# Decay matrices with dt in the exponent, made two heads ahead, in a state-space layer on one Trainium2 core

## The chip, the cores and the metric

One core of one Trainium2 chip runs the program. The time is the device time of one execution in microseconds (us). A run of a kernel is many executions; the table below has the median of three runs. The rows further down come from one execution that the hardware profiler recorded. Engines are named as in the profile: PE (matrix products), PEld (its weight loads), DVE (VectorE), ACT (ScalarE), POOL (GpSimd) and SP (SyncE, which issues the DMAs). Each engine works through its own list of instructions in order.

## What is computed

One layer of a diffusion backbone: 512 tokens with 1024 channels and 256 context tokens. An input projection feeds a convolution module and a bidirectional state-space mixer (SSD); both branches are projected, gated and added, and a squared-ReLU MLP follows. The part that the change touches is, for each direction and each of 32 heads, over chunks of 128 tokens:

```python
cum = jnp.cumsum(dts * a.astype(F32).reshape(g, r), axis=2)
xdt = x5 * dts[..., None]
seg = cum_t[..., :, None] - cum_t[..., None, :]
decay = jnp.exp(jnp.where(lower, seg, -jnp.inf))
cb = jnp.einsum('bcqgn,bckgn->bcgqk', cs_, bs)
y_diag = jnp.einsum('bcgrqk,bckgrp->bcqgrp', cb[:, :, :, None] * decay, xdt)
...
y_off = jnp.einsum('bcqgn,bcgrpn,bcqgr->bcqgrp', cs_, h_in, jnp.exp(cum))
```

`y_diag` needs one 128x128 decay matrix for each head, direction and chunk; `y_off` needs C scaled by exp(cum). In the convolution module the gate is `glu[..., :CONV_DIM] * sigmoid(glu[..., CONV_DIM:])`.

## The kernel before

Channels lie on the partitions, tokens along the rows. Every dense product runs as three passes over high and low parts (`gemm`, lines L114, L115 and L116 of the profile): a weight tile `raw` is loaded by SP, ACT casts it to `whi` (L105), DVE subtracts to get `wlo` (L106), and PE does 24 products of 128x512 for each tile of 128 output channels (128x256 for the context).

Eight groups of four heads follow each other. `proj(g)` makes B, C, x and Z of a group (short convolution on DVE, L374). `ssd(g)` makes B^T C of the four chunks in PSUM (`cps`, L442), two masked copies `cbm` (DVE, L446), B and x by token (L454, L465, L470), the states `sps` on PE (L485) and the scan over chunks `hst` on DVE (L497, L498). Then, for each pair of heads (j) and each head of it (r) and direction (d):

- SP loads `cfb`, two rows of 512 numbers (cum and exp(cum)) spread over all partitions, 512 KB.
- ACT does four Relu (L510) and one Exp (L512) into `e`, DVE multiplies by `cbm` (L513).
- Direction 0: ACT multiplies by dt chunk by chunk (L517). Direction 1: DVE multiplies by dt and adds both directions, four instructions of 128x128 (L520).
- `Cd` = C times exp(cum): on POOL for six of eight in a group, on DVE for direction 0, second head (L523).

PE then does 32 narrow products into `yps` (16 from `Cd` and `hst`, L536, 16 from `e`, L532), DVE finishes `yt` (L540, L541). Products of the next group's projection and of the convolution module stand between these on PE; the convolution's taps run on DVE (L575).

The order in each engine's list is made at build time from a running number in which `later(n)` moves what it holds. Tiles come from pools whose tags have a fixed number of buffers: a tile that takes over a buffer waits for the last reader of the tile that had it. `Cd` of direction 0 has three buffers in the pool `tp`, `Cd` of direction 1 has four in `spool`.

Of the kernel before, what the change touches and what calls it, by code (L numbers as in the profile page):

```python
# [14 lines left out]
P = 128  # L15
# [11 lines left out]
# columns of the packed per-channel vectors  # L27
# [8 lines left out]
# order of the input projection's 128-column tiles  # L36
# [6 lines left out]
# the groups beside which the first tiles of the convolution module run  # L43
GLU_AT = (0, 1, 2, 3, 4)
# [12 lines left out]
def build(tc, xT, ctxT, cond, crow, wada1, wada2, vecs, hv, cst, w_in, w_co, w_so, w_o, w_1, w_2, outT):  # L57
    nc = tc.nc
    with ExitStack() as es:
# [70 lines left out]
        def rsqrt_mean(ps, n, cnt, r=None):  # L130
            """1/sqrt(sum/cnt + EPS) of a sum broadcast over the partitions"""
# [18 lines left out]
        def rsqrt_rows(parts, n, cnt, pool, out=None):  # L150
            """the same of the sum of several tiles, found token by token and then spread over the partitions"""
# [40 lines left out]
        with tc.tile_pool(name="st", bufs=1) as st:  # L192
# [31 lines left out]
            # products of nothing: the tensor engine's clock halves when it idles  # L224
# [52 lines left out]
        nc.sync.dma_start(C[:, 2:], cst[:, 2:])  # L277
# [16 lines left out]
        def dt_part(ps, pc):  # L294
            conv = bigt("conv")
            # rows: heads forward, the same again, heads backward, the same again; the first of each hold
            # chunks 0 to 2, the second chunk 3 and the context
# [40 lines left out]
            nc.vector.tensor_tensor(wg, wg, dt_, ALU.mult)  # L338
            nc.scalar.activation(ecf, cf, AF.Exp)
# [5 lines left out]
            # step s: chunk s forward, chunk 3 - s backward  # L345
# [4 lines left out]
            for src, dst in ((wg, wgT), (cf, cfT), (dt_, dtT)):  # L350
# [36 lines left out]
        def xbc_first():  # L387
            """the first group's, all of x's part before ctx's"""
# [25 lines left out]

        def proj(g):
# [20 lines left out]

        def ssd(g, Bt, Ct, X, Z):
            ch = lambda t, c: t[:, c * P:(c + 1) * P]
            # B^T C of every chunk, for both directions
# [59 lines left out]
            # outputs of the heads, two to a PSUM tile  # L499
            for j in range(2):  # L500
                yps = py.tile([P, T], F32, name="yps", tag="py")
                Ms, Cs = [], ([], [])
                for r in range(2):
                    for d in range(2):
                        hd = d * HEADS + 4 * g + 2 * j + r
                        cb_ = spool.tile([P, 2, T], F32, name="cfb", tag="cfb", bufs=3)
                        nc.sync.dma_start(cb_, s_cf[hd].unsqueeze(0).broadcast_to([P, 2, T]))
                        e = (spool if d else tp).tile([P, T], F32, name="e", tag="e" if d else "M", bufs=2 if d else 3)
                        for c in range(NCH):
                            nc.scalar.activation(  # L510
                                ch(e, c), cb_[:, 0, c * P:(c + 1) * P], AF.Relu, bias=cfT[:, c, hd:hd + 1], scale=-1.0)
                        nc.scalar.activation(e, e, AF.Exp, scale=-1.0)  # L512
                        nc.vector.tensor_tensor(e, e, cbm[d].rearrange("p c q -> p (c q)"), ALU.mult)  # L513
                        if d == 0:
                            M = e
                            for c in range(NCH):
                                nc.scalar.activation(ch(M, c), ch(M, c), AF.Copy, scale=dtT[:, c, hd:hd + 1])  # L517
                        else:
                            for c in range(NCH):
                                nc.vector.scalar_tensor_tensor(  # L520
                                    ch(M, c), ch(e, c), dtT[:, c, hd:hd + 1], ch(M, c), ALU.mult, ALU.add)
# [355 lines left out]
```

## Time and profile before

| | |
|---|---|
| median of 3 runs | 1266.08 us (1263.03 to 1270.63) |
| span of the profiled execution (the page lists no other time of it) | 1264.2 us |
| PE busy | 1220.7 us, 97% of the span |
| DVE busy | 953.7 us, 75% |
| ACT busy | 667.4 us, 53% |
| POOL busy | 108.9 us, 9% |
| stretch of the eight groups | about 97 to 600 us |

Read it so: PE is busy nearly all the time, so its idle time by stretch and what ended it is what a change on other engines can alter. Shares of the whole span hide that DVE's work is not spread evenly over the stages.

### The profile page before, as it was taken

Reading aid. Unit: us, or ns where it says so; the run is one execution under the profiler, and the core shown is the slowest. Engines: PE = TensorE matmul, PEld = TensorE weight load, DVE = VectorE, ACT = ScalarE, POOL = GpSimd, SP = SyncE. Lnnn points to the kernel's source line nnn. Section 1 sums busy time; section 2 is a strip of 40 time slices with the busy share of each in tenths; the row PEclk is TensorE's granted clock in tenths of the full one; section 3 lists DMA queues with packets and bytes.
Section 4 is the critical chain, followed back from the end, with each engine's and each line's share of the span. In section 5 each row is a group of like instructions: output and inputs, shape, how many; then the busy total and the mean of one; then the engine's idle time right before and its main releaser. Section 6 shows DMA issues by size and latency. Waiting matters only on the chain.

```text
span 1264.2 us, 17493 instructions
## 1 busy us (share of the span) xinstructions
PE 1220.7 (97%) x6665; PEld 995.6 (79%) x6665; DVE 953.7 (75%) x1567; ACT 667.4 (53%) x1124; POOL 108.9 (9%) x74
## 2 busy tenths in 40 slices
PE   6998999999999899999999999999999999999997
PEld 3786778777787778787888877778998888888886
DVE  6797689999999999998999798885843343443444
ACT  4557888686776748868453452134431331331442
POOL 0001222121020302124000000000000000000000
PEclk8999999999999999999999999999999999999999
DMA  9424363343342424333363357964222333233332
GB/s 363 142 67 133 137 198 128 120 146 106 121 159 93 158 83 147 112 134 117 109 193 126 119 188 258 305 196 153 62 65 86 100 100 92 92 100 101 96 104 67
DMA packets 56260, 169.96 MB, mean 134 GB/s; under 512 B 6640, under 2 KB 9584, under 8 KB 56048
## 3 DMA queue, kind: packets, MB, share of 16 engines
q1 hardware_dynamic: 56176, 168.85, 41.0%
q8 instruction: 52, 0.85, 0.3%
q14 instruction: 32, 0.26, 0.1%
HBM read 162.27 MB, written 6.55 MB: 134 GB/s over the span
## 4 chain that ended last, share of the span: by engine, by line
PE 65%; DVE 20%; DMA 8%; issue 3%; ACT 3%; SPq 0%; POOL 0%; DVEq 0%; ACTq 0%; POOLq 0%
PE ps L114 20%; PE ps L115 19%; PE ps L116 19%; DVE conv L575 5%; DVE wlo L106 3%; DVE Xt L374 3%; DMA aw<-in_wada_dram 2%; DMA cfb<-s_cf 2%; PE yps L536 2%; PE yps L532 2%; PE sps L485 1%; DMA yr<-s_y 1%; DVE aw L675 1%; DMA raw<-in_w_dram 1%; ACT whi L105 1%
## 5 line engine op out<-in xcount | busy, mean ns | idle before, releaser
L105 ACT CAST whi<-raw 128x1024 fp32r<-128x1024 f32 x163 | 170.9, 1049 | 320.6 <-PE ps L115 291.5
L106 DVE TENSOR_TENSOR wlo<-raw,whi 128x1024 fp32r<-128x1024 f32 x163 | 203.8, 1251 | 84.3 <-ACT whi L105 76.1
L114 PE MATMUL ps<-hh,whi 128*128 128x512 f32 x632 | 258.0, 408 | 2.3 <-DVE Xt L374 2.1
L116 PE MATMUL ps<-hh,wlo 128*128 128x512 f32 x632 | 255.4, 404 | 2.3 <-DVE wlo L106 2.2
L115 PE MATMUL ps<-hl,whi 128*128 128x512 f32 x632 | 256.7, 406 | 0.0
L575 DVE SCALAR_TENSOR_TENSOR conv<-sg,V,conv 128x480 f32<-128x480 f32 (+14 forms) x240 | 173.3, 740 | 2.6 <-ACT conv L569 1.1
L114 PEld LDWEIGHTS ps<-hh,whi 128*128 128x128 f32 x632 | 119.4, 189 | 30.8 <-issue 7.2
L116 PEld LDWEIGHTS ps<-hh,wlo 128*128 128x128 f32 x632 | 119.4, 189 | 30.7 <-DVE wlo L106 4.7
L115 PEld LDWEIGHTS ps<-hl,whi 128*128 128x128 f32 x632 | 119.6, 189 | 26.5 <-issue 3.7
L711 DVE SCALAR_TENSOR_TENSOR x<-ps,mod,x 128x512 f32<-128x512 f32 (+1 forms) x48 | 31.7, 660 | 100.1 <-PE ps L116 100.1
L510 ACT ACTIVATE e<-cfb,cfT 128x128 f32<-128x128 f32 x256 | 83.9, 391 | 36.8 <-PE yps L532 17.5
L523 POOL TENSOR_TENSOR Cd<-Ct,cfb 128x512 f32<-128x512 f32 x48 | 72.6, 1518 | 313.0 <-DMA cfb<-s_cf 250.3
L116 PE MATMUL ps<-h2h,wlo 128*128 128x512 f32 (+1 forms) x240 | 89.8, 375 | 0.0
L115 PE MATMUL ps<-h2l,whi 128*128 128x512 f32 (+1 forms) x240 | 89.8, 375 | 0.0
L114 PE MATMUL ps<-h2h,whi 128*128 128x512 f32 (+1 forms) x240 | 89.4, 375 | 0.0
L115 PE MATMUL ps<-gl,whi 128*128 128x512 f32 x224 | 88.4, 395 | 0.0
L114 PE MATMUL ps<-gh,whi 128*128 128x512 f32 x224 | 88.2, 394 | 0.0
L116 PE MATMUL ps<-gh,wlo 128*128 128x512 f32 x224 | 87.9, 392 | 0.0
L374 DVE SCALAR_TENSOR_TENSOR Xt<-ps,V,Xt 128x255 f32<-128x255 f32 (+3 forms) x128 | 74.2, 605 | 3.9 <-ACT Xt L370 3.6
L114 PE MATMUL ps<-hc,whi 128*128 128x256 f32 x184 | 52.5, 285 | 3.1 <-DVE Xt L374 3.1
L115 PE MATMUL ps<-hc,whi 128*128 128x256 f32 x184 | 52.4, 285 | 0.0
L116 PE MATMUL ps<-hc,wlo 128*128 128x256 f32 x184 | 52.1, 283 | 0.0
(259 smaller groups left out, 2417.5 us busy)
## 6 DMA issues: line engine op xcount, KB each, us to landing
raw<-in_w_in_dram SPq DMA_DIRECT2D x81, 512.0 KB, 3.6
cfb<-s_cf SPq DMA_DIRECT2D x64, 512.0 KB, 4.4
raw<-in_w_dram SPq DMA_DIRECT2D x64, 512.0 KB, 3.5
aw<-in_wada_dram SPq DMA_DIRECT2D x64, 256.0 KB, 4.3
ablk<-in_wada_dram SPq DMA_DIRECT2D x16, 512.0 KB, 8.6
raw<-in_w_so_dram SPq DMA_DIRECT2D x16, 512.0 KB, 3.7
s_y<-yt SPq DMA_DIRECT2D x16, 256.0 KB, 2.2
yr<-s_y SPq DMA_DIRECT2D x16, 256.0 KB, 3.6
```

Of the source, the lines that this page charges most:

```text
L105: nc.scalar.copy(hi, raw)
L106: nc.vector.tensor_tensor(lo, raw, hi, ALU.subtract)
L114: nc.tensor.matmul(ps, lhsT=whi[:, k, :], rhs=rhi[:, k, t0:t1], start=start and k == 0, stop=False)
L115: nc.tensor.matmul(ps, lhsT=whi[:, k, :], rhs=rlo[:, k, t0:t1], start=False, stop=False)
L116: nc.tensor.matmul(ps, lhsT=wlo[:, k, :], rhs=rhi[:, k, t0:t1], start=False, stop=stop and k == KT - 1)
L374: nc.vector.scalar_tensor_tensor(o[:, lo:hi], ps[:, lo + d:hi + d], vcol(V_SCW + 5 * ch + j), o[:, lo:hi], ALU.mult, ALU.add)
L510: nc.scalar.activation(ch(e, c), cb_[:, 0, c * P:(c + 1) * P], AF.Relu, bias=cfT[:, c, hd:hd + 1], scale=-1.0)
L523: (nc.vector if (d, r) in DECAYS_V else nc.gpsimd).tensor_tensor(Cd, Ct, cb_[:, 1, :], ALU.mult)
L532: nc.tensor.matmul(o, lhsT=xt[:, c, hr, :], rhs=ch(Ms[r], c), start=False, stop=True, skip_group_check=True)
L536: nc.tensor.matmul(o, lhsT=hst[:, s, k, hr * 64:hr * 64 + 64], rhs=ch(Cs[k][r], c), start=k == 0 and c == 0, stop=False, skip_group_check= ...
L575: nc.vector.scalar_tensor_tensor(o[:, :, lo:hi], u[:, :, lo + d:hi + d], wv(j), o[:, :, lo:hi], ALU.mult, ALU.add)
L711: nc.vector.scalar_tensor_tensor(x1[:, j, a:b], ps[:, a:b], mod[:, gcol + j, 0:1], x1[:, j, a:b], ALU.mult, ALU.add)
```

## The change

- `expo` makes the decay matrices by itself, two heads ahead of use (`LEAD = 2`). For each head and direction it loads only the cum row (`E`, 256 KB, L459 of the changed kernel). POOL's `affine_select` writes -1e30 outside the triangle (L463), ACT does four Exp with the bias `bT` = ln(dt) - cum (no Relu, no multiplication by dt), DVE adds the two directions (L468) and, at use, multiplies by `cb`, an unmasked copy of B^T C that ACT makes (L541, L478).
- `Cd` has a DMA of its own for the exp(cum) row, which lands in the `Cd` tile (L537) and is multiplied in place (L538), by POOL or DVE as before. Direction 1 has seven buffers, direction 0 still three.
- `cbm` and the masks are gone, and one of three transposed dt tables; DVE and ACT do a max, a Ln and a subtraction in its place.
- The gate of the convolution is tanh: ACT does Tanh(0.5 x), DVE (tanh + 1) times a, and 0.5 goes into the tap weights once.

```diff
+CDB, EB, LEAD, ADDV, E_LATER, E_LATER0 = 7, 7, 2, 1, 0, 0
...
+            nc.vector.tensor_scalar(dt_, dt_, DT_MIN, None, ALU.max)
+            nc.scalar.activation(dt_, dt_, AF.Ln)
+            nc.vector.tensor_tensor(dt_, dt_, cf, ALU.subtract)
...
-            for src, dst in ((wg, wgT), (cf, cfT), (dt_, dtT)):
+            for src, dst in ((wg, wgT), (dt_, bT)):
...
+        def expo(upto):
...
+                for d in range(2):
+                    hd = d * HEADS + h
+                    e = (tp if d else spool).tile([P, T], F32, name="E", tag="M" if d else "E", bufs=3 if d else EB)
+                    nc.sync.dma_start(e, s_cf[hd, 0].unsqueeze(0).broadcast_to([P, T]))
...
+                    x3 = e.rearrange("p (c q) -> p c q", q=P)
+                    sign = -1 if d else 1
+                    nc.gpsimd.affine_select(x3, x3, pattern=[[0, NCH], [sign, P]], compare_op=ALU.is_ge,
+                                            fill=never, base=0, channel_multiplier=-sign)
+                    for c in range(NCH):
+                        nc.scalar.activation(x3[:, c], x3[:, c], AF.Exp, bias=bT[:, c, hd:hd + 1])
+                    es_.append(e)
+                (nc.vector if ADDV else nc.gpsimd).tensor_tensor(es_[0], es_[0], es_[1], ALU.add)
+                ahead.append(es_[0])
...
-            cbm = []
-            for m in (mask_f, mask_b):
...
+            cb = spool.tile([P, T], F32, name="cb", tag="cb", bufs=1)
+            nc.scalar.copy(cb, cps)
...
-                        cb_ = spool.tile([P, 2, T], F32, name="cfb", tag="cfb", bufs=3)
-                        nc.sync.dma_start(cb_, s_cf[hd].unsqueeze(0).broadcast_to([P, 2, T]))
...
-                        Cd = (spool if d else tp).tile([P, T], F32, name="Cd", tag="Cd", bufs=4 if d else 3)
-                        (nc.vector if (d, r) in DECAYS_V else nc.gpsimd).tensor_tensor(Cd, Ct, cb_[:, 1, :], ALU.mult)
+                        Cd = (spool if d else tp).tile([P, T], F32, name="Cd", tag="Cd", bufs=CDB if d else 3)
+                        nc.sync.dma_start(Cd, s_cf[hd, 1].unsqueeze(0).broadcast_to([P, T]))
+                        (nc.vector if (d, r) in DECAYS_V else nc.gpsimd).tensor_tensor(Cd, Ct, Cd, ALU.mult)
                         Cs[d].append(Cd)
+                    M = ahead.pop(0)
+                    nc.vector.tensor_tensor(M, M, cb, ALU.mult)
                     Ms.append(M)
+                with later(E_LATER):
+                    expo(4 * g + 2 * j + 2 + LEAD)
...
-                nc.scalar.activation(sg, pb, AF.Sigmoid)
+                nc.scalar.activation(sg, pb, AF.Tanh, scale=0.5)
...
-                nc.vector.tensor_tensor(sg, sg, pa, ALU.mult)
+                nc.vector.scalar_tensor_tensor(sg, sg, 1.0, pa, ALU.add, ALU.mult)
```

The order moves at three places that matter below. First, POOL's list at its start, group 0. Before, its first instructions are the `Cd` of the first heads:

```order
L523 TENSOR_TENSOR Cd_1024<-Ct_586,cfb_1011 128x512 [waits DMAHW0_49]
L523 TENSOR_TENSOR Cd_1054<-Ct_586,cfb_1041 128x512 [waits DMAHW2_49]
L523 TENSOR_TENSOR Cd_1099<-Ct_586,cfb_1086 128x512 [waits DMAHW4_49,PE_49]
L523 TENSOR_TENSOR Cd_1114<-Ct_586,cfb_1101 128x512 [waits DMAHW5_49]
L523 TENSOR_TENSOR Cd_1144<-Ct_586,cfb_1131 128x512 [waits DMAHW7_49]
L523 TENSOR_TENSOR Cd_1664<-Ct_1251,cfb_1651 128x512 [waits DMAHW0_49,PE_49,Activation_49]
L523 TENSOR_TENSOR Cd_1679<-Ct_1251,cfb_1666 128x512 [waits DMAHW3_49,PE_49,Pool_49]
```

In the changed kernel seven `affine_select` stand ahead of six `Cd` (the last three of the seven are shown), and two more behind them:

```order
L463 AFFINE_SELECT E_955<-E_955 128x512 [waits DMAHW1_49]
L463 AFFINE_SELECT E_962<-E_962 128x512 [waits DMAHW2_49,DVE_49]
L463 AFFINE_SELECT E_970<-E_970 128x512 [waits DMAHW3_49]
L538 TENSOR_TENSOR Cd_1052<-Ct_587,Cd_1052 128x512 [waits DMAHW3_49,Activation_49]
L538 TENSOR_TENSOR Cd_1055<-Ct_587,Cd_1055 128x512 [waits DMAHW4_49]
L538 TENSOR_TENSOR Cd_1062<-Ct_587,Cd_1062 128x512 [waits DMAHW7_49]
L538 TENSOR_TENSOR Cd_1096<-Ct_587,Cd_1096 128x512 [waits DMAHW1_49,PE_49]
L538 TENSOR_TENSOR Cd_1099<-Ct_587,Cd_1099 128x512 [waits DMAHW2_49]
L538 TENSOR_TENSOR Cd_1106<-Ct_587,Cd_1106 128x512 [waits DMAHW3_49]
L463 AFFINE_SELECT E_1110<-E_1110 128x512 [waits DMAHW4_49]
L463 AFFINE_SELECT E_977<-E_977 128x512 [waits DMAHW5_49,DVE_49]
```

So the first heads' `Cd`, and the last `E` of the first group, come behind more work on POOL.

Second, DVE's list at the first chunk scan of group 0 (`hst`), before:

```order
L470 TENSOR_TENSOR xw1_949<-xps_957,wgT_575 128x256
L470 TENSOR_TENSOR xw0_948<-xps_965,wgT_575 128x256 [waits PE_49]
L470 TENSOR_TENSOR xw1_949<-xps_965,wgT_575 128x512
L497 TENSOR_TENSOR hst_973<-hst_973,decb_576 128x512 [waits DMAHW5_49,Activation_49]
L498 TENSOR_TENSOR hst_973<-hst_973,sps_980 128x512 [waits DVE_49,PE_49]
L497 TENSOR_TENSOR hst_973<-hst_973,decb_576 128x512 [waits DVE_49]
L498 TENSOR_TENSOR hst_973<-hst_973,sps_985 128x512 [waits DVE_49,PE_49]
```

and in the changed kernel:

```order
L541 TENSOR_TENSOR E_940<-E_940,cb_990 128x512
L381 SCALAR_TENSOR_TENSOR Xt_1283<-ps_1314,V_72,Xt_1283 128x254 [waits DVE_49]
L468 TENSOR_TENSOR E_970<-E_970,E_977 128x512 [waits DMAHW3_49,DMAHW5_49,Activation_49,Pool_49]
L541 TENSOR_TENSOR E_955<-E_955,cb_990 128x512
L541 TENSOR_TENSOR E_970<-E_970,cb_990 128x512 [waits DVE_49]
L527 TENSOR_TENSOR hst_1029<-hst_1029,decb_574 128x512 [waits DMAHW6_49,Activation_49]
L111 TENSOR_TENSOR wlo_1416<-raw_1413,whi_1415 128x1024 [waits DMAHW0_49,PE_49,Activation_49]
L528 TENSOR_TENSOR hst_1029<-hst_1029,sps_1036 128x512 [waits DVE_49,PE_49]
```

The scan's first step now stands behind the sum of a head's two directions (which waits for POOL and ACT) and two products with `cb`.

Third, PE's list at the second pair of heads of group 2, where `Cd` of direction 0, second head, takes over the buffer of the first pair's first `Cd` (three buffers, four tiles in a group; names end in the tile's number). Before, the last product that reads the old tile, `Cd_2321`, is the fifth of these rows:

```order
L536 MATMUL yps_2307<-Cd_2321,hst_2285 64x128 [waits DVE_49]
L536 MATMUL yps_2307<-Cd_2351,hst_2285 64x128
L536 MATMUL yps_2307<-Cd_2321,hst_2285 64x128 [waits DVE_49]
L536 MATMUL yps_2307<-Cd_2351,hst_2285 64x128
L536 MATMUL yps_2307<-Cd_2321,hst_2285 64x128 [waits DVE_49]
L536 MATMUL yps_2307<-Cd_2351,hst_2285 64x128
```

and the first that reads the new tile, `Cd_2443`, comes 97 instructions after it, here last but one:

```order
L114 MATMUL ps_2604<-hh_76,whi_2599 128x512
L115 MATMUL ps_2604<-hl_77,whi_2599 128x512
L116 MATMUL ps_2604<-hh_76,wlo_2600 128x512
L114 MATMUL ps_2604<-hh_76,whi_2599 128x512
L536 MATMUL yps_2399<-Cd_2443,hst_2285 64x128 [waits DVE_49]
L536 MATMUL yps_2399<-Cd_2413,hst_2285 64x128
```

In the changed kernel the old tile is `Cd_2266`, read last in the third of these rows:

```order
L555 MATMUL yps_2265<-Cd_2266,hst_2243 64x128 [waits DVE_49]
L555 MATMUL yps_2265<-Cd_2273,hst_2243 64x128
L555 MATMUL yps_2265<-Cd_2266,hst_2243 64x128 [waits DVE_49]
L555 MATMUL yps_2265<-Cd_2273,hst_2243 64x128
L555 MATMUL yps_2265<-Cd_2269,hst_2243 64x128 [waits Pool_49]
L555 MATMUL yps_2265<-Cd_2276,hst_2243 64x128 [waits Pool_49]
```

and the new one, `Cd_2349`, is read first in the last of these:

```order
L555 MATMUL yps_2341<-Cd_2342,hst_2243 64x128 [waits Pool_49]
L119 MATMUL ps_2424<-hh_76,whi_2419 128x512
L120 MATMUL ps_2424<-hl_77,whi_2419 128x512
L121 MATMUL ps_2424<-hh_76,wlo_2420 128x512
L119 MATMUL ps_2424<-hh_76,whi_2419 128x512
L120 MATMUL ps_2424<-hl_77,whi_2419 128x512
L121 MATMUL ps_2424<-hh_76,wlo_2420 128x512
L119 MATMUL ps_2424<-hh_76,whi_2419 128x512
L555 MATMUL yps_2341<-Cd_2349,hst_2243 64x128 [waits DVE_49]
```

So 25 instructions lie between, 18 narrow ones into `yps` and seven products, where there were 97. SP's list at the new tile's load:

```order
L101 DMA raw_2485<-in_w_in_dram 128x1024 [waits DMAHW4_49,DVE_49]
L101 DMA raw_2523<-in_w_in_dram 128x1024 [waits DMAHW5_49,DVE_49]
L537 DMA Cd_2349<-s_cf_575 128x512 [waits PE_49,Pool_49]
L537 DMA Cd_2889<-s_cf_575 128x512 [waits PE_49]
L101 DMA raw_2591<-in_w_in_dram 128x1024 [waits DMAHW1_49,DVE_49]
```

and DVE's at its product:

```order
L594 SCALAR_TENSOR_TENSOR conv_717<-sg_2133,V_72,conv_717 128x8x49 [waits Activation_49]
L594 SCALAR_TENSOR_TENSOR conv_717<-sg_2133,V_72,conv_717 128x8x50 [waits DVE_49]
L559 SCALAR_TENSOR_TENSOR yt_2334<-Xt_1906,V_72,yps_2265 128x512 [waits PE_49]
L538 TENSOR_TENSOR Cd_2349<-Ct_1868,Cd_2349 128x512 [waits DMAHW3_49,Pool_49]
L560 TENSOR_TENSOR yt_2334<-yt_2334,Z_2067 128x512 [waits DVE_49]
L594 SCALAR_TENSOR_TENSOR conv_717<-sg_2133,V_72,conv_717 128x8x51
```

The load itself now waits for PE's last use of the old tile. Before, the numbers came in `cfb`, which has buffers of its own, and only the product waited for the old tile.

## Rows read from the trace of the kernel before

**Rows 1.** The page: span, and busy time of each engine.

```profile
span 1264.2 us, 17493 instructions
PE 1220.7 (97%) x6665; PEld 995.6 (79%) x6665; DVE 953.7 (75%) x1567; ACT 667.4 (53%) x1124; POOL 108.9 (9%) x74
```

**Rows 2.** Windows: stretch and length, busy of PE, PEld, DVE, ACT, POOL; clock; DMA.

```profile
97.00:200.00 103.00, 94.83 (x582) 73.82 (x581) 77.47 (x135) 85.41 (x182) 18.90 (x14) 0.98 0.49 154
200.00:600.00 400.00, 389.74 (x2309) 315.26 (x2309) 383.35 (x618) 292.24 (x542) 81.68 (x52) 1.00 0.38 126
114.00:120.00 6.00, 6.00 (x29) 4.00 (x27) 3.69 (x6) 4.74 (x9) 2.59 (x2) 0.72 0.29 99
129.00:136.00 7.00, 6.18 (x45) 5.05 (x46) 5.53 (x13) 5.76 (x12) 2.07 (x2) 1.00 0.09 37
```

**Rows 3.** What PE waited for, 97 to 200 us: total, times, longest.

```profile
PE yps L536 <- POOL Cd L523: 6.2, 3, 3.1
PE dtp L353 <- DVE conv L338: 1.6, 1, 1.6
```

**Rows 4.** Timeline of PE and POOL in group 0.

```profile
113.69 0.43 PE L536 MATMUL yps<-Cd,hst 128*64 128x128 f32 x2 [3.15 <-POOL Cd L523]
129.82 0.43 PE L536 MATMUL yps<-Cd,hst 128*64 128x128 f32 x2 [1.65 <-POOL Cd L523]
112.37 2.96 POOL L523 TENSOR_TENSOR Cd<-Ct,cfb 128x512 f32<-128x512 f32 x2 [111.92 <-DMA cfb<-s_cf]
```

**Rows 5.** What PE waited for, 200 to 600 us.

```profile
PE ps L114 <- DVE Xt L374: 3.4, 2, 2.1
PE ps L116 <- DVE wlo L106: 2.1, 3, 0.9
PE sps L485 <- DVE xw L470: 1.2, 2, 0.8
PE yps L536 <- DVE hst L498: 1.1, 3, 0.5
```

**Rows 6.** Groups by form: count, busy us, mean ns of one, idle ahead.

```profile
L520 DVE SCALAR_TENSOR_TENSOR e<-e,dtT 128x128 f32<-128x128 f32 x128 | 42.6, 358 | 0.2
L446 DVE TENSOR_TENSOR cbm<-cps,C 128x512 f32<-128x512 f32 x16 | 10.4, 682 | 1.6 <-PE cps L442 1.4
L218 DVE TENSOR_SCALAR xr<-xr,mod 128x512 f32<-128x512 f32 x8 | 4.2, 543 | 0.6 <-ACT hh L217 0.6
```

**Rows 7.** The tile cfb: readers' durations, minimum, median, maximum ns; landing of its DMA.

```profile
L523 POOL TENSOR_TENSOR Cd<-Ct,cfb x48: 1264/1304/3853, 112.4 to 594.0; 128x512 f32<-128x512 f32 x48
L523 DVE TENSOR_TENSOR Cd<-Ct,cfb x16: 678/684/1778, 114.8 to 593.4; 128x512 f32<-128x512 f32 x16
DMA to landing us min/median/max: 3.3/4.4/7.6
```

**Rows 8.** Timeline of POOL and DVE at 276 us.

```profile
276.53 3.08 POOL L523 TENSOR_TENSOR Cd<-Ct,cfb 128x512 f32<-128x512 f32 x2 [13.86 <-ACT Ct L384]
279.57 1.64 POOL L548 TENSOR_TENSOR yacc<-yacc,ysq 128x512 f32<-128x512 f32 x1
276.78 3.28 DVE L575 SCALAR_TENSOR_TENSOR conv<-sg,V,conv 128x408 f32<-128x408 f32 x2
279.99 1.78 DVE L523 TENSOR_TENSOR Cd<-Ct,cfb 128x512 f32<-128x512 f32 x1
```

**Rows 9.** DMA issues, KB each and median us to landing; then the tile yr's landing.

```profile
yr<-s_y SPq DMA_DIRECT2D x16, 256.0 KB, 3.6
DMA to landing us min/median/max: 2.5/3.6/3.9
```

**Rows 10.** Timeline of PE: two products in a row, and sixteen narrow ones.

```profile
122.85 0.39 PE L114 MATMUL ps<-hh,whi 128*128 128x512 f32 x1
123.08 0.39 PE L115 MATMUL ps<-hl,whi 128*128 128x512 f32 x1
532.47 1.04 PE L532 MATMUL yps<-e,xt 128*64 128x128 f32 x16
```

More of the change, by code (lines that the diff above doesn't have):

```diff
@@ L41 @@
 NW_IN = W_GATE + 16
-GLU_AT = (0, 1, 2, 3, 4)
+GLU_AT = tuple(range(5))
 BEGIN_AT, CTX_AT = (0, 1, 2), 3
@@ L67, in build @@
         V = cp.tile([P, NV], F32, name="V")
-        C = cp.tile([P, 4, P], F32, name="C")
-        ident, ones, mask_f, mask_b = (C[:, i, :] for i in range(4))
+        C = cp.tile([P, 2, P], F32, name="C")
+        ident, ones = (C[:, i, :] for i in range(2))
         def bigt(name, dt=F32, shape=(P, KT, T)):
@@ L285, in build @@
         H2 = 2 * HEADS
-        cfT = cp.tile([P, NCH, H2], F32, name="cfT")
-        dtT = cp.tile([P, NCH, H2], F32, name="dtT")
+        bT = cp.tile([P, NCH, H2], F32, name="bT")
         wgT = cp.tile([P, NCH + 2, H2], F32, name="wgT")
@@ L413, in build @@
         cacc = acct("cacc")
+        nc.vector.tensor_scalar(V[:, V_DWW:], V[:, V_DWW:], 0.5, None, ALU.mult)
+        never = nc.gpsimd.to_reg(NEVER)
         def proj(g):
@@ L435, in bc @@
             return ap.unsqueeze(len(shape) - 1).broadcast_to(shape)
+        ahead = []
+        asked = [0]
+        def expo(upto):
+            while asked[0] < min(upto, HEADS):
+                h = asked[0]
+                asked[0] += 1
+                es_ = []
+                for d in range(2):
[11 more added lines that the diff above has]
+                ahead.append(es_[0])
         def ssd(g, Bt, Ct, X, Z):
@@ L505, in ssd @@
                         hd = d * HEADS + 4 * g + 2 * j + r
-                        cb_ = spool.tile([P, 2, T], F32, name="cfb", tag="cfb", bufs=3)
-                        nc.sync.dma_start(cb_, s_cf[hd].unsqueeze(0).broadcast_to([P, 2, T]))
[L508 to L521, printed above, removed]
-                        Cd = (spool if d else tp).tile([P, T], F32, name="Cd", tag="Cd", bufs=4 if d else 3)
-                        (nc.vector if (d, r) in DECAYS_V else nc.gpsimd).tensor_tensor(Cd, Ct, cb_[:, 1, :], ALU.mult)
+                        Cd = (spool if d else tp).tile([P, T], F32, name="Cd", tag="Cd", bufs=CDB if d else 3)
+                        nc.sync.dma_start(Cd, s_cf[hd, 1].unsqueeze(0).broadcast_to([P, T]))
+                        (nc.vector if (d, r) in DECAYS_V else nc.gpsimd).tensor_tensor(Cd, Ct, Cd, ALU.mult)
                         Cs[d].append(Cd)
+                    M = ahead.pop(0)
+                    nc.vector.tensor_tensor(M, M, cb, ALU.mult)
                     Ms.append(M)
+                with later(E_LATER):
+                    expo(4 * g + 2 * j + 2 + LEAD)
                 for k in range(3):
@@ L584, in build @@
         cur = proj(0)
+        with later(E_LATER0):
+            expo(2 + LEAD)
         for g in range(G):
@@ L837, in _layout @@
             inp["conv_dw_w"][0].reshape(CK, 8, P).transpose(2, 1, 0).reshape(P, -1)]
-    i = np.arange(P)
-    cst = np.stack([np.eye(P), np.ones((P, P)), i[:, None] <= i[None, :], i[:, None] >= i[None, :]], 1)
+    cst = np.stack([np.eye(P), np.ones((P, P))], 1)
     return {
```

6 lines of the change are left out of this document (1 added, 5 removed).

## The prediction

> **What bounds the kernel now.** The page first: PE is busy 1220.7 us of a span of 1264.2, DVE 75% [rows 1]. Then the windows by stage, because DVE's share is uneven: from 200 to 600 us, where seven of the eight groups run, PE is busy 389.74 us of 400 and DVE 383.35, that is 96%; ACT has 292.24 and POOL 81.68 [rows 2]. So PE bounds the stage and DVE is close behind. Only PE's idle time can be won. From 97 to 200 it is 103 − 94.83 = 8.2 us, from 200 to 600 it is 400 − 389.74 = 10.3 us, 18.5 together. The waits say by whom: in group 0 (and the start of group 1) POOL's `Cd` for 6.2 us in three waits, and the dt part for 1.6 [rows 3]; later DVE's evictions and low weight parts, 3.4 + 2.1 + 1.2 + 1.1 = 7.8 us in rows and 2.5 in smaller ones [rows 5]. Last the clock: behind the 3.15 us wait at 113.69 [rows 4] PE is busy all of the six microseconds from 114, at 0.72 of full clock, so 6 × 0.28 = 1.7 us are lost, while behind the wait of 1.65 us at 129.82 the window shows 1.00 [rows 2, 4]. A second loss of that size lies behind the later wait of 2.1 us, if it goes the same way (an estimate from the first). The ceiling of what the change can win is 18.5 + 3.4 = about 22 us.
>
> **DVE's load.** Gone are 128 instructions of dt times e (42.6 us) and 16 masked copies (10.4 us) [rows 6]. The 64 products with the mask stay as many: 32 sums and 32 products with `cb`, same shape, no change. A max, a subtraction and one scaling of the tap weights cost about 1.9 us (three of at most 0.68, all in the first row's class of cost [rows 6]). That is −51 us. Against it stand 64 `affine_select` on POOL, which no row shows. Bounds for one: 0.54 us, DVE's one-input instruction of this size [rows 6], and 1.3 to 1.5 us, POOL's two-input product (median 1.30, 3.08/2 in the timeline [rows 7, 8]). I take 1.0, the middle.
>
> POOL's work costs DVE time. From 276.53 to 281.2 POOL works 4.7 us, and two taps of 128x408 and one product of 128x512 take DVE 3.28 + 1.78 = 5.06 us; with 0.68 for an undisturbed product [rows 7] and as much at most for a tap, the work is 2.0 us, so 3.0 us are lost, 0.65 for each of POOL's [rows 8]. That is the worst case, in which every DVE instruction reads two tiles of SBUF; the other bound is 0, since evictions read PSUM. I take a third: 64 × 1.0 × 0.33 = 21 us. The net is −51 + 21 = −30 us on DVE, near 4 us per group; bounds −51 and 64 × 1.5 × 0.65 − 51 = +11.
>
> The Trainium skill ("SBUF — State Buffer", Who interferes with whom) says that a DVE instruction with two SBUF inputs and a GpSimd instruction that reads SBUF exclude each other on a shared port pair for the whole instruction; the two-input rows at 276 us agree, and no row shows an `affine_select`. By it each one could hold DVE up for all its length, 64 us by my middle price, and the change would add 13 us to DVE's work where my sum takes 30 away.
>
> What a lighter DVE gives PE: the 10.3 us of idle from 200 to 600 and 1.7 of clock are nearly all DVE's lateness. A stretch with 4 us per group of slack should lose most, not all (a wait for a chain, product to eviction to product, does not care about load): I take −7, bounds 0 and −12.
>
> **Group 0.** The order puts 55 products of 512 columns and 24 of 256 columns more ahead of the first `yps`: 55 × 0.23 + 24 × 0.12 = 15.5 us of cover (0.23 is the distance of two products [rows 10], 0.12 half of it). The waits of 6.2 and 1.6 and the 1.7 of clock go, 9.5 us [rows 3]. But a new chain ends late: POOL's seven `affine_select`, six `Cd`, two `affine_select` are 9 × 1.0 + 6 × 1.3 = 17 us, starting, I estimate, 6 to 8 us before the 112.4 at which its first `Cd` started [rows 4], since the loads of `E` are issued ahead; then four Exp, the sum of two directions, two products, the scan's product, a low weight part and the scan's sum on DVE, about 6 us with 0.68 for each 128x512. End near 128 to 129. PE stands at the first `yps` at 113.69 − 3.15 − 1.56 + 15.5 = 124.5 [rows 3, 4] and wants the scan's step a microsecond later: a wait of about 3.5 us and again 1.7 of clock. Sum −9.5 + 5.2 = −4; bounds −9.5 and +6 (`affine_select` at 1.5 adds 4.5 us and more behind it).
>
> **A wait that is new.** In each group four `Cd` of direction 0 share three buffers, so the fourth takes that of the first. Now its DMA starts only when PE has read the first for the last time. From there PE has 18 narrow products (1.04/16 = 0.065 each) and seven wide ones of 0.23 [rows 10]: 1.2 + 1.6 = 2.8 us until it wants the new tile. That needs landing plus DVE's product, 0.68 [rows 7]. For the landing I take 3.6 us, the median of the 256 KB of `yr`; bounds 2.5, its fastest [rows 9], and 4.4, the median of the 512 KB of `cfb`, from the same source [rows 7]. Wait: 3.6 + 0.68 − 2.8 = 1.5 us, 0.4 to 2.3. The order shows the same 24 to 28 rows between in all eight groups: +12 us, 3 to 18. At 2.3 us the clock would fall each time as behind 3.15, 8 × 1.7 = 14 more, 32 in all. Before, 97 instructions lay between in group 2, and only the last group had so few. Queued behind that DMA on SP are the next group's `Cd` and a weight tile; behind the product on DVE, `yt`'s second step and the taps, which lose the same 1.5 us, 12 of the 30 won.
>
> **At nothing.** ACT loses a Relu pass, a dt pass and most changes of function table; it has 108 us free of the 400 [rows 2] and PE's list waits for it in no row shown. The DMA bytes are the same (64 × 512 KB against 128 × 256 KB); 64 more issues stay on SP. The exponentials of later groups are ready a group ahead, so a late `affine_select` there hurts only through DVE; without that lead each would stand in the chain for `yps`. PE loses three transposes, −0.4. Before 97 and after 600 us the order is the same.
>
> **Sum.** +12 − 4 − 7 − 0.4 = +0.6: a span of 1264.8. The median of the runs stands 1.9 above the profiled span; so about 1266.7, I say 1267.
>
> **Rivals.**
> 1. Slower: POOL takes DVE over. It decides at 64 × price × share = 51, that is 0.8 us lost for each `affine_select`. For it: 0.65 lost per POOL microsecond in the timeline [rows 8]. Against: the second operand is missing. At 1.5 × 0.65 DVE gets 11 us more where it has 16.6 us free in 400: the −7 turns to about +6, group 0 to +2, the new wait stays: 1266 + 20 = 1286; at 1.2 us and half that, 1278.
> 2. Faster: the load lands in 2.5 us, so the new wait is 3 us in all. For it: half the bytes of `cfb`, and nothing else is issued just then. Against: the median of 3.6. Then 3 − 4 − 7 = −8, and with −10 from DVE −11: 1255 to 1258.
> 3. Much faster: that, and no wait is left but a few: −9.5 − 11 + 3 = −17, 1249 or less.
> 4. The new wait is above 2 us and the clock falls behind it: +32 − 11 = +21, 1287.
>
> **How the numbers follow.** Chances: forecast 0.42 (1259 to 1275), rival 1 0.18, rival 2 0.27, rival 3 0.07, rival 4 0.06. Half a per cent, 6.3 us, is about what a measurement of this kernel tells from no change, so 1259.8 and 1272.4 are the limits. Of the forecast 0.32 lies between them, 0.03 below and 0.07 above; of rival 2 0.23 below and 0.04 between. Faster 0.03 + 0.23 + 0.07 = 0.33, same 0.36, slower 0.07 + 0.18 + 0.06 = 0.31. The range leaves out most of rival 3, a third of rival 1 and rival 4: 1251 to 1284.
>
> **What would show it.** PE's waits: eight for `Cd` from DVE at the second pair, 1.5 us each, with a DMA behind DVE's idle time; no wait for POOL's `Cd` in group 0, and one for `hst` of 3 to 4 us near 125; fewer for `Xt` and `wlo`. `affine_select` near 1.0 us; DVE's busy time from 200 to 600 down by 20 to 30 us. The forecast is wrong if an `affine_select` holds DVE up by 0.8 us or more, if the new `Cd` loads land in under 3 us, or if the waits for `Xt` and `wlo` do not care about DVE's load.

## The result and the profile after

The changed kernel takes 1251.3 us (median of 4 runs, 1248.84 to 1252.88); the kernel before has 1265.12 with its run of the same chip. The ratio is 0.9893, 95% interval 0.9865 to 0.9921: some 14 us faster. The forecast was 1267, no change; 1251.3 lies at the very edge of the range. The profiled run of the changed kernel is the fastest of its four (1248.84), so the two spans below differ by 17.2 us where the medians differ by 14.

The page's busy rows, answering to [rows 1]:

```profile
span 1247.0 us, 17404 instructions
PE 1202.9 (96%) x6662; PEld 995.0 (80%) x6662; DVE 924.0 (74%) x1426; ACT 545.2 (44%) x900; POOL 173.4 (14%) x138
```

Subtract before looking for waits. PE's idle time was 1264.2 − 1220.7 = 43.5 us and is now 1247.0 − 1202.9 = 44.1. It has not fallen. PE's *busy* time has, by 17.8 us, although PE has only 3 instructions fewer of 6665. The whole gain of the span, 17.2 us, lies there. DVE's busy time fell by 29.7.

What PE waited for from 97 to 600 us (total, times, longest), answering to [rows 3, 5]:

```profile
PE yps L555 <- DVE Cd L538: 5.2, 8, 1.4
PE sps L515 <- ACT xt L507: 4.3, 1, 4.3
PE ps L121 <- DVE wlo L111: 3.6, 5, 0.7
PE xps L495 <- ACT Bk L485: 2.3, 4, 1.2
```

The waits changed their names and not their sum: those for `Cd` on POOL are gone, those for evictions have shrunk, those for low weight parts have grown (3.6 us where [rows 5] has 2.1), and eight waits for the reloaded `Cd`, one long one in group 0 and some for ACT have come.

Where did PE's busy time go? The timeline of PE in the kernel before, one place in group 2 where narrow products (32-bit float, for `yps`) stand between wide ones (the rounded 32-bit format that `gemm` uses); columns are start, length, instruction, count:

```profile
249.57 0.38 PE L532 MATMUL yps<-e,xt 128*64 128x128 f32 x2
249.79 0.38 PE L536 MATMUL yps<-Cd,hst 128*64 128x128 f32 x2
250.10 0.50 PE L114 MATMUL ps<-hh,whi 128*128 128x512 f32 x1
250.44 0.40 PE L115 MATMUL ps<-hl,whi 128*128 128x512 f32 x1
250.68 0.40 PE L116 MATMUL ps<-hh,wlo 128*128 128x512 f32 x1
```

No wait is printed anywhere, yet the starts are not even: the first wide product takes 250.44 − 250.10 = 0.34 us of PE's time and the next ones 0.23. The changed kernel, one pair of heads of group 3:

```profile
310.30 0.39 PE L120 MATMUL ps<-hl,whi 128*128 128x512 f32 x1
310.52 0.39 PE L121 MATMUL ps<-hh,wlo 128*128 128x512 f32 x1
310.84 1.97 PE L555 MATMUL yps<-Cd,hst 128*64 128x128 f32 x32
312.64 1.04 PE L551 MATMUL yps<-E,xt 128*64 128x128 f32 x16
313.51 0.38 PE L555 MATMUL yps<-Cd,hst 128*64 128x128 f32 x2
313.82 0.50 PE L119 MATMUL ps<-hh,whi 128*128 128x512 f32 x1
314.16 0.39 PE L120 MATMUL ps<-hl,whi 128*128 128x512 f32 x1
```

Here all the products of a pair stand together. (There are 24 of them, not 32 as the text ahead of the prediction says, and the profile records each twice: 32 + 16 records. The two records at 313.51 are the first product of the next pair.) Going in costs 310.84 − 310.52 = 0.32 where a wide product takes 0.23, and coming out costs again, so each *visit* of PE to narrow products between wide ones seems to have a fixed price. In the trace PE goes from another product to a narrow one 66 times before and 23 times after (63 and 20 times from a wide one). 17.8 / 43 = 0.41 us for one, at most: the clock has a part in the 17.8 too (see the table of all kernels).

### The profile page after: what moved, and what is told of

The parts are those of the page before. It is cut to its first block, busy times and chain, and to the rows that moved or that the text cites. A ratio compares the mean times of both kernels' runs of the same rounds, so it can differ in the third digit from the quotient of the medians.

```text
span 1247.0 us, 17404 instructions
## 1 busy us (share of the span) xinstructions
PE 1202.9 (96%) x6662; PEld 995.0 (80%) x6662; DVE 924.0 (74%) x1426; ACT 545.2 (44%) x900; POOL 173.4 (14%) x138
## 4 chain that ended last, share of the span: by engine, by line
PE 59%; DVE 21%; DMA 10%; ACT 4%; issue 3%; POOL 1%; SPq 0%; DVEq 0%; ACTq 0%; POOLq 0%
PE ps L119 18%; PE ps L121 18%; PE ps L120 17%; DVE conv L594 7%; DVE wlo L111 3%; PE sps L515 3%; DMA Cd<-s_cf 3%; DVE Xt L381 3%; DMA aw<-in_wada_dram 2%; PE yps L555 1%; DMA E<-s_cf 1%; DVE Ct L381 1%; DMA yr<-s_y 1%; DVE Bt L381 1%; POOL E L463 1%
## 5 line engine op out<-in xcount | busy, mean ns | idle before, releaser
L119 PE MATMUL ps<-hh,whi 128*128 128x512 f32 x632 | 255.2, 404 | 2.5 <-DVE Bt L381 1.7
L120 PE MATMUL ps<-hl,whi 128*128 128x512 f32 x632 | 253.7, 401 | 0.0
L594 DVE SCALAR_TENSOR_TENSOR conv<-sg,V,conv 128x392 f32<-128x392 f32 (+14 forms) x240 | 181.7, 774 | 1.8
L466 ACT ACTIVATE E<-E,bT 128x128 f32<-128x128 f32 x256 | 79.8, 393 | 35.7 <-POOL E L463 35.5
L538 POOL TENSOR_TENSOR Cd<-Ct,Cd 128x512 f32<-128x512 f32 x48 | 76.6, 1624 | 84.4 <-ACT Ct L391 70.1
L463 POOL TENSOR_SCALAR_AFFINE_SELECT E<-E 128x512 f32<-128x512 f32 x64 | 61.7, 979 | 182.5 <-DVE Bt L381 100.5
L381 DVE SCALAR_TENSOR_TENSOR Xt<-ps,V,Xt 128x510 f32<-128x510 f32 (+3 forms) x128 | 74.3, 605 | 4.3 <-ACT Xt L377 3.9
```

The costliest lines, as they stand in the source:

```text
L119: nc.tensor.matmul(ps, lhsT=whi[:, k, :], rhs=rhi[:, k, t0:t1], start=start and k == 0, stop=False)
L120: nc.tensor.matmul(ps, lhsT=whi[:, k, :], rhs=rlo[:, k, t0:t1], start=False, stop=False)
L381: nc.vector.scalar_tensor_tensor(o[:, lo:hi], ps[:, lo + d:hi + d], vcol(V_SCW + 5 * ch + j), o[:, lo:hi], ALU.mult, ALU.add)
L463: nc.gpsimd.affine_select(x3, x3, pattern=[[0, NCH], [sign, P]], compare_op=ALU.is_ge, fill=never, base=0, channel_multiplier=-sign)
L466: nc.scalar.activation(x3[:, c], x3[:, c], AF.Exp, bias=bT[:, c, hd:hd + 1])
L538: (nc.vector if (d, r) in DECAYS_V else nc.gpsimd).tensor_tensor(Cd, Ct, Cd, ALU.mult)
```

## The experiments

Two theories. **V**: the gain is that PE makes 43 visits fewer. **D**, the prediction's own: a lighter DVE makes PE wait less. Times are medians with the ratio to the kernel before, run on the same chip.

**Gather the products in the kernel before.** The decay matrices, which come last, are asked for first:

```diff
-                for k in range(3):
-                    for c in range(NCH):
-                        for r in range(2):
+                for k in (2, 0, 1):
+                    for c in (range(NCH) if k < 2 else (3, 2, 1, 0)):
+                        for r in ((0, 1) if k < 2 else (1, 0)):
...
-                                                 start=False, stop=True, skip_group_check=True)
+                                                 start=c == 3, stop=False, skip_group_check=True)
...
-                                                 start=k == 0 and c == 0, stop=False, skip_group_check=True)
+                                                 start=False, stop=k == 1, skip_group_check=True)
```

> The kernel before, with one edit: the sixteen products of the decay matrices come first in a pair of heads, from the last chunk back, and those of Cd behind them, so that PE starts a pair when all its matrices are there. DVE, ACT, POOL and the DMAs have the same work. PE's list then goes from wide to narrow products 16 times where it went 66 times. Theory V (each such visit costs PE some 0.4 us beyond its products, worked out from the spacing of products in the two traces): 50 x 0.4 = 20 us less, 1245, and perhaps 5 us of it given back by waits for the last matrix: 1245 to 1252. Theory D (the gain of the change comes from a lighter DVE): no change, 1260 to 1270.

1244.26 us, ratio 0.9837 (0.9804 to 0.9871). Its page:

```profile
span 1240.3 us, 17506 instructions
PE 1198.3 (97%) x6665; PEld 998.2 (80%) x6665; DVE 956.7 (77%) x1567; ACT 670.1 (54%) x1127; POOL 109.1 (9%) x74
```

DVE is as full as before, and the order of PE's products alone wins 20 us, 22.4 of them in PE's busy time. V holds; D can't explain it.

**Scatter them in the changed kernel**, the loops of the narrow products giving way to 30 instructions:

```diff
-                for k in range(3):
-                    for c in range(NCH):
+                with later(30):
+                    for k in range(3):
+                        for c in range(NCH):
...
```

> The changed kernel, with one edit: the narrow products give way to the next 30 instructions in the order of priority, so that PE's list goes from wide to narrow products 97 times where it went 23 times. All other work is the same. Theory V: 74 x 0.4 = 30 us more, about 1280. Theory D: no change from the changed kernel's 1251, or a little less, since a product that comes later waits less.

1272.28 us, ratio 1.0064 (1.0043 to 1.0085), 21 us slower than the changed kernel. PE is busy 1230.8 us of 1270.5: +27.9 for 74 visits, 0.38 each; its idle time fell by 4.4 to 39.7, as theory D allowed for products that come later. That is why 21 and not 30.

**The price by itself.** 256 narrow products more in the MLP, where PE runs wide products alone. The edit, within `gemm`, for two behind every third pass (sixteen behind the last for the second run; for the third run the operands are `whi[:, k, :64]` and `rhi[:, k, :P]`, and the output lies in the first 64 partitions):

```diff
+                if extra[0] is not None and k in range(KT):
+                    for i in range(2):
+                        nc.tensor.matmul(extra[0][64 * (i % 2):64 * (i % 2) + 64, :P], lhsT=ones[:, :64], rhs=ident,
+                                         start=True, stop=True, skip_group_check=True)
```

> The price of a visit by itself, in the MLP, where PE has wide products alone and waits for nobody: the changed kernel with 256 narrow products more (64 columns of weights, 128 columns moved, 32-bit float, results not used), two behind every third pass of the products of two quarters, so 128 visits of two. Theory V: 256 x 0.054 = 14 us for the products, 128 x 0.36 = 46 us for the visits: 1251 + 60 = 1311. If a visit costs nothing where nobody waits (theory D): 1265.

> The same 256 narrow products, sixteen behind each tile's wide ones: 16 visits. Theory V: 14 + 16 x 0.4 = 20 us: 1271, 40 less than with visits of two. Theory D: the same as with visits of two.

> Visits of two again, but the narrow products have the number format of the wide ones (the rounded 32-bit format of the high and low parts) and take 64 columns of the weights and 128 of the tokens from the same tiles. If the price of a visit is one of the small shape (a short product can't cover the next weight load), it stays near 46 us: 1300 to 1311. If it is one of the change of number format, it goes: 1251 + 14 to 20 = 1265 to 1271.

1326.24, 1283.63 and 1277.2 us, ratios 1.0493 (1.0453 to 1.0534), 1.0156 (1.0127 to 1.0185) and 1.0105 (1.0074 to 1.0136). The first two do the same products; 112 visits more take 42.6 us: **0.38 us for a visit** by the medians of two runs each, 0.35 by PE's busy time in the two traces (1276.8 and 1237.5). PE in the run with visits of two:

```profile
1000.15 0.40 PE L123 MATMUL ps<-h2h,wlo 128*128 128x512 f32 x1
1000.48 0.44 PE L126 MATMUL junk<-C 128*64 128x128 f32 x4
1000.85 0.50 PE L121 MATMUL ps<-h2h,whi 128*128 128x512 f32 x1
1001.18 0.39 PE L122 MATMUL ps<-h2l,whi 128*128 128x512 f32 x1
1001.41 0.40 PE L123 MATMUL ps<-h2h,wlo 128*128 128x512 f32 x1
```

and with the same number format on both sides:

```profile
1000.37 0.40 PE L123 MATMUL ps<-h2h,wlo 128*128 128x512 f32 x1
1000.60 0.28 PE L126 MATMUL junk<-h2h,whi 128*64 128x128 f32 x2
1000.72 0.44 PE L121 MATMUL ps<-h2h,whi 128*128 128x512 f32 x1
1001.00 0.39 PE L122 MATMUL ps<-h2l,whi 128*128 128x512 f32 x1
1001.23 0.39 PE L123 MATMUL ps<-h2h,wlo 128*128 128x512 f32 x1
```

Read the distances of starts. In the first, 0.33 (in), 0.37 (two products, each recorded twice, and the way out), 0.33 (first wide one), then 0.23. In the second, 0.23, 0.12, 0.28, then 0.23: going in is free and 0.05 is left on the way out. So 64 columns of weights alone do not make the price, since both runs share them. The number format alone doesn't either. The kernel before has float products with all 128 columns of weights between wide ones, here those of the states:

```profile
309.53 0.59 PE L485 MATMUL sps<-xw,Bk 128*128 128x256 f32 x2
309.77 0.58 PE L115 MATMUL ps<-hl,whi 128*128 128x512 f32 x1
310.19 0.59 PE L485 MATMUL sps<-xw,Bk 128*128 128x256 f32 x2
310.43 0.58 PE L116 MATMUL ps<-hh,wlo 128*128 128x512 f32 x1
```

From 309.53 to 310.19 one float and one wide product take 0.66 us. The wide one is 0.23, and 0.43 is also what a float product of this shape takes among its own kind (two records, 0.215 us apart in this trace), so the two changes of format cost next to nothing. The price needs both, float and the narrow shape.

All three totals came out higher than expected: 15 and 13 us in the first two, because a float product leaves two records and costs 0.11, where I had taken one record, 0.054, for the whole of it; the third lies 6 us above its range, far below the 1300 that the small shape alone would have made.

**Take the new wait away**: `Cd` of the second head from direction 1's seven buffers.

```diff
-                        Cd = (spool if d else tp).tile([P, T], F32, name="Cd", tag="Cd", bufs=CDB if d else 3)
+                        Cd = (spool if d or r else tp).tile([P, T], F32, name="Cd", tag="Cd", bufs=CDB if d or r else 3)
```

> The changed kernel, with one edit: Cd of direction 0, second head, takes its buffers from the seven that direction 1 has, so no Cd load waits for a product of the same group. The eight waits of PE for that Cd (5.2 us in the trace) should go by both theories: -5 us. The visits go from 23 to 15: theory V has 3 us more to win. V: 1243; D: 1246 to 1248. If the waits only move to another operand, 1251.

1243.0 us, ratio 0.9825 (0.9795 to 0.9855). No wait for `Cd` is left; PE's idle time fell only from 44.1 to 42.3, its busy time by 2.9 to 1200.0 with 15 visits. In this trace waits moved on to the low weight parts (5.7 us where 3.6 stood) and the states' products (5.4 where 4.3 stood, and 1.7 where 0.6), while the profiled spans differ by 4.7 us and the medians by 8; which of the two is nearer is within the runs' scatter.

**Give DVE its work back** in the changed kernel: four instructions of 128x128 in place of one of 128x512, at both places.

```diff
-                (nc.vector if ADDV else nc.gpsimd).tensor_tensor(es_[0], es_[0], es_[1], ALU.add)
+                for c in range(NCH):
+                    o = slice(c * P, (c + 1) * P)
+                    nc.vector.scalar_tensor_tensor(es_[0][:, o], es_[0][:, o], 1.0, es_[1][:, o], ALU.mult, ALU.add)
...
-                    nc.vector.tensor_tensor(M, M, cb, ALU.mult)
+                    for c in range(NCH):
+                        nc.vector.scalar_tensor_tensor(ch(M, c), ch(M, c), 1.0, ch(cb, c), ALU.mult, ALU.mult)
```

> The changed kernel, with DVE's relief taken back: the sum of the two directions and the product with B^T C are done by four instructions of 128x128 each in place of one of 128x512. At 0.36 us against 0.68 for the whole that is 64 x (4 x 0.36 - 0.68) = +48 us on DVE, as much as the change took away. The visits stay, 22 for 23. Theory V (visits): 1251 to 1256, since some waits for DVE come back. Theory D (DVE): the gain is gone, 1262 to 1268.

1264.47 us, ratio 1.0006 (0.9992 to 1.0021): D's number, with V's visits unchanged at 22. So V is not the whole truth. DVE's busy time rose by 17.5 us, of the 29.7 that the change had taken. PE's busy time rose by 4.2 only, to 1207.1; its idle time rose from 44.1 to 56.1. The waits from 97 to 600 us:

```profile
PE xps L497 <- ACT Bk L487: 8.1, 4, 2.1
PE yps L558 <- DVE Cd L540: 6.0, 8, 1.7
PE ps L121 <- DVE wlo L111: 4.4, 6, 0.7
PE sps L517 <- ACT xt L509: 3.9, 1, 3.9
```

PE's idle time in these groups grew by 10.3 us (19.6 to 29.9). 5.8 of that is ACT's copy of B by token, most of the rest is spread over operands that DVE makes. Of the 4.2 in busy time the lower clock has more than all (see the table). ACT does its instructions in order, and it waited 56.5 us for `affine_select` where it waited 35.5 in the changed kernel; why POOL came later there was not tested. This kernel, unlike the kernel before, has a chain DMA, POOL, ACT, DVE for each matrix in the engines' lists, and, as far as these waits show, needs DVE light enough to keep it moving.

**Leave POOL's part out.** The 64 `affine_select` are dropped and Exp takes a fixed scale without bias.

```diff
-                    nc.gpsimd.affine_select(x3, x3, pattern=[[0, NCH], [sign, P]], compare_op=ALU.is_ge,
-                                            fill=never, base=0, channel_multiplier=-sign)
...
-                        nc.scalar.activation(x3[:, c], x3[:, c], AF.Exp, bias=bT[:, c, hd:hd + 1])
+                        nc.scalar.activation(x3[:, c], x3[:, c], AF.Exp, scale=1e-3)
```

> The changed kernel without the 64 affine_select; the Exp has a small scale and no bias, so that it stays finite. Left out: the triangle and the exponent of the decay matrices; the values of the SSD branch are others, the shapes and all other instructions are the same, visits 23. It measures what POOL's part costs the others. By the trace of the changed kernel a product of 128x512 on DVE takes 0.87 us beside POOL and 0.685 without: with 62 us of POOL gone DVE is 15 to 20 us lighter. Theory V: waits alone can fall, 1247 to 1251. If POOL's work on the shared path is what limits the change: 1240 or less.

1239.08 us, ratio 0.9811 (0.9782 to 0.9839): 12 us less than the changed kernel. PE's busy time is 1201.0, near the same; its idle time falls from 44.1 to 38.3; the wait of 4.3 us in group 0 is gone, and of those for ACT's copies 0.2 us are left. DVE's busy time falls from 924.0 to 909.1, 0.23 us for each `affine_select`. The time is below V's 1247 to 1251, and in the range put down for a limit by POOL's work.

**The gate alone**, on the kernel before:

```diff
-                nc.scalar.activation(sg, pb, AF.Sigmoid)
+                nc.scalar.activation(sg, pb, AF.Tanh, scale=0.5)
...
-                nc.vector.tensor_tensor(sg, sg, pa, ALU.mult)
+                nc.vector.scalar_tensor_tensor(sg, sg, 1.0, pa, ALU.add, ALU.mult)
...
+        nc.vector.tensor_scalar(V[:, V_DWW:], V[:, V_DWW:], 0.5, None, ALU.mult)
```

> The kernel before with the tanh gate alone. DVE has the same number of instructions and one small one more; ACT loses some changes of function table. The order of PE's list shifts all the same: 45 visits where there were 66. Theory V: 21 x 0.4 = 8 us less, about 1257. Theory D: no change, 1263 to 1267.

1264.05 us, ratio 0.9987 (0.9972 to 1.0003): a miss for V. PE's busy time fell by 3.0 only, and its idle time rose by 4.9 to 48.4; the profiled span, 1266.1, is above its own median. The clock hides a part of V's gain: between 100 and 1250 us this trace shows four stretches at half clock where the kernel before has two, and 3.8 us more of PE's busy time go to it; without that the busy time fell by 6.8. Fewer visits are worth their price only while no waits take their place.

**The gate undone**, in the changed kernel: the same edit backwards.

```diff
-                nc.scalar.activation(sg, pb, AF.Tanh, scale=0.5)
+                nc.scalar.activation(sg, pb, AF.Sigmoid)
...
```

> The changed kernel with the sigmoid gate of before in place of tanh. Visits 23 as with tanh, DVE one small instruction less, ACT some changes of function table more. Theory V and theory D alike: 1251 within half a per cent. If the tanh gate carries part of the gain, above 1255.

1252.3 us, ratio 0.9915 (0.9889 to 0.9942): the gate carries nothing that can be measured.

**Fewer visits still.** On the kernel with `Cd` from the common pool, direction 1's products first, and apart from it the gathered order of the first experiment:

```diff
-                for k in range(3):
+                for k in (1, 2, 0):
...
-                                                 start=False, stop=True, skip_group_check=True)
+                                                 start=k == 1 and c == 0, stop=k == 0, skip_group_check=True)
...
```

> The kernel of the run with Cd from the common pool, with one edit more: the products of direction 1 come first in a pair, then the decay matrices', then direction 0. The visits go from 15 to 8. Theory V: 7 x 0.4 = 3 us less than 1243, about 1240, if no wait takes its place; theory D: 1243.

> The two edits that won most, together: Cd of the second head from the common pool, and the decay matrices' products first in a pair. Visits 13 where the run with the pool alone had 15. Theory V: 1 us less than that, 1242, if the waits stay as they are. The run with direction 1 first had fewer visits and more waits: 1253 would be that again.

1253.12 us, ratio 0.9923 (0.9898 to 0.9948), with 8 visits, and 1244.04, ratio 0.9858 (0.9821 to 0.9895), with 13. With 8 PE waited 54.0 us in all against 42.3, with ACT's Exp (6.5 us in the groups) and the scan of the states (4.0 us) named high in the list: each pair now asks for the last state of the scan at once. So the run with 8 visits misses both expectations, 1240 and 1243, and the one with 13 comes within 2 us of V's 1242. The spans of the three, 1242.3, 1253.4 and 1238.8, all have PE busy within 2.2 us of each other; the waits decide. The gathered kernel of before, 1244, and the changed one with `Cd` from the common pool, 1243, are the best of these and can't be told apart.

The kernels side by side (visits counted in the trace; busy and idle from the page of each):

| kernel | visits | span | PE busy | PE idle | lost at half clock |
|---|---|---|---|---|---|
| before | 66 | 1264.2 | 1220.7 | 43.5 | 7.9 |
| before, gathered | 16 | 1240.3 | 1198.3 | 42.0 | 7.9 |
| before, tanh | 45 | 1266.1 | 1217.7 | 48.4 | 11.7 |
| changed | 23 | 1247.0 | 1202.9 | 44.1 | 4.9 |
| changed, sigmoid | 23 | 1250.3 | 1206.6 | 43.7 | 8.4 |
| changed, scattered | 97 | 1270.5 | 1230.8 | 39.7 | 6.1 |
| changed, DVE's work back | 22 | 1263.2 | 1207.1 | 56.1 | 11.1 |
| changed, no affine_select | 23 | 1239.3 | 1201.0 | 38.3 | 6.3 |
| changed, Cd from the pool | 15 | 1242.3 | 1200.0 | 42.3 | 8.5 |
| that, direction 1 first | 8 | 1253.4 | 1199.4 | 54.0 | 9.4 |
| that, gathered | 13 | 1238.8 | 1197.8 | 41.0 | 6.6 |

Busy time also holds products at a lower clock, so rows with the same visits differ by up to 6 us. The last column is half of PE's busy time in the stretches that each trace shows at half clock (0.5, the level of 1.2 GHz). From the kernel before to the changed one it falls by 3.0 us, part of it in the start, where both do the same work; so 14.8 of the 17.8 us are left for the 43 visits, 0.34 each. Take the column off the busy time, and all eleven kernels lie within 2.7 us of 1186.6 + 0.40 x visits (a line fitted to this table). So theory V accounts for PE's busy time in every kernel here, and not for the waits: DVE's work back adds 12 us of them and 6.2 at half clock to the changed kernel with one visit fewer (some 5 us of the two before 97 us, where both kernels do the same work). The gain is the visits'; by that run, a lighter DVE is what keeps it from being lost to waits.

## Why the prediction was wrong, point by point

**What bounds the kernel.** "Only PE's idle time can be won" is the step that failed. PE's idle time went from 43.5 to 44.1, and the sum said +0.6, but that is luck: the new wait brought 5.2 us where +12 stood; from 97 to 200 us, apart from the 1.8 of it that fall there, idle time fell by 1.2 (8.2 to 8.8 in all) where −4 stood; from 200 to 600, apart from its other 3.4, it fell by 2.8 (10.3 to 10.8 in all) where −7 stood with the clock. The 17.8 us came out of PE's busy time, for which the sum had no term but three transposes and the clock; what the runs showed in its place is a price of some 0.4 us for each visit to narrow products, 43 of which went. The traces of before held it: in [rows 4] a narrow product stands alone between wide ones, and the order, read for what each place waits for, was never read for how often PE changes its kind of product, nor the timeline for the distance of two starts where the kind changes.

**DVE's load.** Right in size: −30 predicted, 953.7 to 924.0 measured. An `affine_select` was taken at 1.0 us:

```profile
L463 POOL TENSOR_SCALAR_AFFINE_SELECT E<-E 128x512 f32<-128x512 f32 x64 | 61.7, 979 | 182.5 <-DVE Bt L381 100.5 <-DMA E<-s_cf 81.6
```

0.98. Its hold on DVE was taken as a third of it, 0.33; leaving it out gave 0.23. The Trainium skill ("SBUF — State Buffer", Who interferes with whom) would have a DVE instruction with two SBUF inputs shut out by it for its whole length; on the mean of all DVE instructions the runs show a quarter of that. The step from DVE's load to PE's waits stays half open: the waits for evictions fell (3.4 us for `Xt` before, 1.7 for `Bt` and `Ct` after), those for low weight parts rose from 2.1 to 3.6, and the kernel with DVE's work back lost 13 us, but more through ACT's copies behind POOL than through the evictions that the prediction named.

**Group 0.** −4 predicted. The waits for POOL's `Cd` and the clock's loss behind them went, the wait for the dt part fell from 1.6 to 1.0, and a new one of 4.3 us came, 3.5 predicted, with the clock's loss of 1.7 behind it as predicted (0.72 of full clock from 126 to 132). Its place was near: 125.99 us, where I had PE at 124.5. It is ACT's copy of x that PE waits for; ACT stood behind four Exp that waited 4.44 us for POOL:

```profile
124.19 1.28 ACT L466 ACTIVATE E<-E,bT 128x128 f32<-128x128 f32 x4 [4.44 <-POOL E L463]
125.37 1.04 ACT L507 COPY xt<-xps 128x512 f32<-128x512 f32 x2
```

So a late POOL was the right cause; ACT's list was the one queued behind it, and not DVE's scan. That the time fits is luck in part. POOL began at 99.74, 5 to 7 us earlier than estimated, and then stood for 9.2 us waiting for loads of `Cd`, for which the sum of POOL's work (17 us) had nothing:

```profile
110.56 2.52 POOL L538 TENSOR_TENSOR Cd<-Ct,Cd 128x512 f32<-128x512 f32 x2 [5.24 <-DMA Cd<-s_cf]
116.26 1.30 POOL L538 TENSOR_TENSOR Cd<-Ct,Cd 128x512 f32<-128x512 f32 x1 [3.18 <-DMA Cd<-s_cf]
118.30 4.23 POOL L538 TENSOR_TENSOR Cd<-Ct,Cd 128x512 f32<-128x512 f32 x3 [0.75 <-DMA Cd<-s_cf]
```

**A wait that is new.** It came, eight times, from the operand and at the place named, and was mis-sized: +12 predicted, 5.2 measured. The cover was miscounted. 1.04/16 = 0.065 is the price of a record, and each narrow product leaves two; the 18 products take 2.3 us and not 1.2, the cover is 3.9. One instance in the changed kernel, SP's issue, DVE's product and PE's first use:

```profile
312.01 0.80 SPq L537 DMA_DIRECT2D Cd<-s_cf  x2
315.56 0.69 DVE L538 TENSOR_TENSOR Cd<-Ct,Cd 128x512 f32<-128x512 f32 x1 [0.62 <-DMA Cd<-s_cf]
316.31 1.85 PE L555 MATMUL yps<-Cd,hst 128*64 128x128 f32 x29 [0.59 <-DVE Cd L538]
```

The load takes 3.5 us (3.0 to 3.6 in the eight; 3.6 taken), the product 0.69 (0.68 taken). From 130 to 1230 us, behind all eight of these waits, the granted clock is 1.00, so the dearer bound, with the clock, did not come.

**At nothing.** ACT's and the gate's parts, right: the sigmoid version measures the same. That ACT's list is never waited for was not: 7.3 us of waits now carry its name.

**The rivals.** None named the mechanism. The time lies between the second and the third, which were to be faster through shorter waits. The first, POOL taking DVE over, was put at more than it is: all of POOL's part costs 12 us, measured.

## What to carry to other kernels

Where PE is the bound, compare its busy time before its waits: here each visit to float products with 64 columns of weights between rounded ones with 128 had a price of some 0.4 us, while rounded products of the narrow shape and float ones of the full width had hardly any; so a list that collects the products of the dear kind was worth more than many small waits. A change that makes operands ready earlier also changes the order of the engine that uses them; read the new order for how the kinds alternate, and not only for what each place waits for. Count a profile's records against the loops that issue them before pricing by one.

## What the runs showed of the hardware that was not expected

- A visit of PE to 32-bit float products with 64 columns of weights between rounded 32-bit ones with 128 cost 0.35 to 0.4 us beyond the products, with nothing waited for. With both in the rounded format it was some 0.05 to 0.1, and float products with 128 columns in the same place (the states', above) cost next to nothing beyond themselves. The Trainium skill ("TensorEngine Tiling (Array Packing)", Key Properties) says that a change of tiling mode drains TensorE. If going from 128 to 64 columns of weights is such a change, this agrees with both kinds of float product and not with the rounded ones. Why those go nearly free, and whether the price is a matter of the weight load or of the product, was not tried.
- Four instructions of 128x128 on DVE in place of one of 128x512 took 80.2 us where 49.4 stood, 31 more, but added only 17.5 to DVE's busy time: the rest of its work became 13 us shorter. Why was not tried.
